# A hybrid decoder layer: a one-column GpSimd copy behind a mask product, half a low part moved from an adding transfer to VectorE, and five smaller moves of order and buffers

## The chip, the cores and the metric

The kernel runs on one core of a Trainium2 chip. The metric is the time of one execution in microseconds on the device, as the median of the runs. Its engines are TensorE (PE, matrix products), VectorE (DVE), ScalarE (ACT), GpSimd (POOL) and SyncE (SP, which only issues transfers); each has its own queue of instructions and they wait for each other by semaphores.

## What is computed

One step of a decoder layer for a prompt of 512 tokens and eight samples of eight tokens each, which share all weights. Cut to what matters here:

```python
def hybrid_layer(x, ...):
    u = _rms(x) * g_pre_mix
    proj = u @ w_in                       # 1024 -> z, xbc, dt, q, k, v, ig, fg, og
    xbc, conv_new = causal_conv(xbc, conv_buf, conv_w, conv_b)
    xs, bm, cm = split(silu(xbc))
    y_ssd, h_new = ssd_scan(xs, dt, a, bm, cm, h_ssm)      # Mamba2
    y_ssd = _rms((y_ssd + d_skip * xs) * silu(z)) * g_ssm_out
    h_ml, c_new, n_new, m_new = mlstm_scan(q, k, v, i_pre, logf, mc, mn, mm)
    h_ml = _rms(h_ml) * g_mlstm_out * sigmoid(og)
    x = x + _rms(concat([y_ssd, h_ml]) @ w_out) * g_post_mix
    o = softmax((_rms(x) * g_pre_x @ w_xq) @ mem_k.T / 16) @ mem_v @ w_xo
    x = x + _rms(o) * g_post_x
    f = (silu(u @ w_gate) * (u @ w_up)) @ w_down           # u = _rms(x) * g_pre_ffn
    return x + _rms(f) * g_post_ffn, ...
```

In `ssd_scan` the weights of one chunk are `cb * exp(segment sums, masked) * dt`; the states `h` of the samples are scaled by their decay and get one outer product added.

## The kernel before

Tokens lie in columns: 576 of them, as halves of 256 and 320. Every float32 weight tile of 128 x 1024 is split into a high part (`whi`, a cast) and a low part (`wlo`, the weight less the high part), and every product is three: high times high, high times the low part of the input, low times high (lines 208, 209 and 211 for most). A scheduler sets the order of each engine's instructions from the order of the code; `tc.issue_after(x)` places what is inside behind `x` in that order, without adding a wait of its own. An engine waits where the data or a buffer demand it.

The places that the change touches, in order of time:

- **Start** (lines 306 to 350). `NWARM` products on zeros run on TensorE while the first loads come. SP issues `par` (a table of scales), then for each of eight steps pieces of two weight tiles (`raw`) and of the input (`xraw`). ScalarE makes `uh`, the scaled input's high part, VectorE `ul`.
- **Input tiles.** `split_w` (line 178) loads a tile to `raw`, casts it on ScalarE and makes the low part: columns up to `cut` by a subtraction on VectorE, the rest, where `acc` is set, by ScalarE writing the negated high part to `wlo` and a transfer on GpSimd's queue that adds the weight to it from memory. `in_tile` (line 393) calls it by `fetch`. `conv_tile(j)` uses `in_tile(1 + j, ev, 0)`: cut 0, all by the adding transfer. `gate_tile` (line 433) runs ahead of `conv_tile(4)`, which takes input tile 5: it copies 40 rows twice out of each PSUM buffer (`xg`, `la`) on ScalarE.
- **Rows** (lines 520 to 620). Cumulated sums of the gates as rows, `cum`, `gpr`, `sx`, which TensorE then transposes (`ps_ct`). Copies in bfloat16 pieces go to `cumst` and `sxst`; `d1t` is what is left after a piece.
- **Chunk masks** (`ssd_prompt`, line 622). For each pair of heads `j`: TensorE spreads a row over PSUM (`ps_l`), VectorE adds the column term and the mask in four instructions (line 670), ScalarE takes the exponential, VectorE multiplies by `cbs` (line 673, listed in `mults`), and TensorE uses both masks of the pair in `ps_yi`. Meanwhile, in the code that follows, GpSimd scales the samples' states (`h`, line 789, two of 128 x 1024 for each `b`), after TensorE has read them for `ps_hs`; for `b == 2` that call stands in `issue_after(mults[7])`. The masks `mults[6]` and `mults[7]` are those of `j=3` in the first group.
- **z tiles** (`z_evac`, line 1050): VectorE multiplies a z tile's PSUM by the norm's row, first half and second half.
- **Memory weights** (`wm_split`): four more tiles are loaded to the shared `raw` buffers, of which there are two, and split.
- **Output projection of the attention** (`xo`, line 1529). Eight tiles for the first half of the columns, each in a PSUM buffer of the pool `pg`, which has three in turn; weights are in three `whi`/`wlo` buffers. An evacuation is a square and a sum (`add_sq`) and a scaled copy to `f_xo`, both on ScalarE but for the sum. Tile `j` takes its buffers behind the evacuation of tile `j - 3`.

Of the kernel before, what the change touches and what calls it, by code (L numbers as in the profile page):

```python
# [11 lines left out]
F32 = mybir.dt.float32  # L12
F32R = mybir.dt.float32r
BF16 = mybir.dt.bfloat16
AF = mybir.ActivationFunctionType
ALU = mybir.AluOpType
# [3 lines left out]
P = 128  # L20
# [4 lines left out]
KT = 8  # L25
# [81 lines left out]

CUT = 512
CCUT = 128
NWARM = 21  # L110
NSS = 7
NWX = 3
TCOPT = dict(schedule_with_timeline_sim=True)
# [2 lines left out]
def build(nc, tc, ctx, I, O):  # L116
# [190 lines left out]
    psw = MP("ps_warm")  # L307
    for _ in range(NWARM):
        mm(psw[:, 0:256], wz[:, 0:128], wz, start=True, stop=True, skip_group_check=True)
    S.dma_start(par, I["par"])  # L310

    wl = [wp.tile([P, 1024], F32R, name="wlo", tag="wlo", bufs=3) for _ in range(2)]
    RT = {k: wp.tile([P, 3], F32, name=k + "_r", tag=k + "_r") for k in ("px0", "p30", "px1", "p31")}
# [2 lines left out]
    for k in range(KT):  # L316
        if k % 2 == 0:
            c = slice(128 * k, 128 * k + 256)
            S.dma_start(raws[0][:, c], I["win"][1][:, c])
        xd = (S if k else A).dma_start(xraw[:, k, :], I["xT"][:, k, :])  # L320
        if k % 2 == 0:
            xd = (S if k else A).dma_start(raws[1][:, c], I["win"][2][:, c])
        if k == 0:
            with tc.issue_after(xd.ins), tc.high_priority(offset=300):

                A.activation(sp.tile([P, 1], F32, name="one"), wz[:, 0:1], AF.Exp)

        if k == 0:
            V.tensor_copy(wi[0][0][:, c], raws[0][:, c])
        for t0, n in ([(0, T)] if k else HALVES):  # L330
            ts_ = slice(t0, t0 + n)
            uhk = A.activation(uh[:, k, ts_], xraw[:, k, ts_], AF.Copy, scale=PAR("g_pre", k))
            ulk = V.scalar_tensor_tensor(ul[:, k, ts_], xraw[:, k, ts_], PAR("g_pre", k), uh[:, k, ts_].bitcast(F32),
                                         op0=ALU.mult, op1=ALU.subtract)
        if k % 2 == 0:
            for i in range(2):
                with tc.issue_after(uhk.ins), tc.issue_after(ulk.ins):
                    split(wi[i][0][:, c], wi[i][1][:, c], raws[i][:, c], cast=None if k or i else lambda *_: None)
# [123 lines left out]
    def conv_tile(j, dst):  # L462

        cb = cv.tile([P, 604], F32, name="cb", tag="cb", bufs=2)
        sm = cb[:, CS:CB].rearrange("p (b t) -> p b t", t=11)

        def ev(t0, n, ps):
            V.tensor_tensor(cb[:, 3 + t0:259 + t0], ps[:, 0:256], rxb[:, t0:t0 + 256], op=ALU.mult)
            if t0:
                V.tensor_tensor(sm[:, :, 3:11], ps[:, 256:320].rearrange("p (b t) -> p b t", t=8),  # L470
                                rxb[:, TP:T].rearrange("p (b t) -> p b t", t=8), op=ALU.mult)

        in_tile(1 + j, ev, 0)
        with ExitStack() as after:
            if 4 <= j < 10:
                for i in range(2 + j, 4 + j):
                    if i > last_in[0]:
                        fetch(i, 0)
                        last_in[0] = i
                after.enter_context(tc.issue_after(accs[-1].ins))  # L480
            if late_rows:
                late_rows.pop()()
            G.memset(cb[:, 0:3], 0.0)
            G.tensor_copy(sm[:, :, 0:3], cst[:, j, :, :])

        def rows_out():
            G.tensor_copy(convo[:, j, 0:3], cb[:, CS - 3:CS])
            G.tensor_copy(convo[:, j, 3:27].rearrange("p (b t) -> p b t", t=3), sm[:, :, 8:11])

        late_rows.append(rows_out)  # L490
        e = V
        ac = cv.tile([P, 604], F32, name="ac", tag="ac", bufs=2)
        A.activation(ac[:, 0:600], cb[:, 0:600], AF.Identity, scale=PAR("convw", 4 * j), bias=PAR("convb", j))
        for k in range(1, 4):
            e.scalar_tensor_tensor(ac[:, 0:600], cb[:, k:600 + k], PAR("convw", 4 * j + k), ac[:, 0:600],
                                   op0=ALU.mult, op1=ALU.add)
        A.activation(dst[:, 0:TP], ac[:, 0:TP], AF.Silu)
        sa = ac[:, CS:CB].rearrange("p (b t) -> p b t", t=11)
        A.activation(dst[:, TP:T].rearrange("p (b t) -> p b t", t=8), sa[:, :, 0:8], AF.Silu)
# [58 lines left out]
    V.tensor_copy(mp[r4, 512:576].rearrange("p (c t) -> p c t", t=8), m0.unsqueeze(2).to_broadcast([4, 8, 8]))  # L558
    sx = row("sx", tag="la")
    V.tensor_tensor(sx[r4, :], cum[r4, :], mrw[r4, :], op=ALU.subtract)  # L560
    V.tensor_tensor(sx[r4, :], sx[r4, :], mp[r4, :], op=ALU.add)
    V.tensor_tensor(gpr[r4, :], ig[r4, :], cum[r4, :], op=ALU.subtract)
    V.tensor_tensor(gpr[r4, :], gpr[r4, :], mp[r4, :], op=ALU.subtract)
    r2 = row("r2", 4, tag="i2")
# [7 lines left out]
    for st_, src, n in ((cumst, cum[0:16, :], 16), (sxst, sx[r4, :], 4)):  # L572
        b0 = 32 if n == 4 else 0
        bt, d1 = btt[b0:b0 + n, :], d1t[b0:b0 + n, :]
        G.memset(st_, 0.0)
        V.tensor_copy(bt, src)
        A.copy(st_[0:n, :], bt)
        V.tensor_tensor(d1, src, bt, op=ALU.subtract)
        V.tensor_copy(bt, d1)
        A.copy(st_[32:32 + n, :], bt)  # L580
        V.tensor_tensor(d1, d1, bt, op=ALU.subtract)
        A.copy(st_[64:64 + n, :], d1)
# [41 lines left out]
    def ssd_prompt(g):  # L624
# [35 lines left out]
        for j in range(4):  # L660
# [3 lines left out]
            for k in range(2):  # L664
                h = 2 * jj + k
                psb = MP("ps_l")
                mm(psb, sel[:80, h:h + 1].to_broadcast([80, P]), cumst[:, 0:TP], start=True, stop=True)
                lm = sd.tile([P, 512], F32, name="lm", tag="tmp", bufs=2)
                for c in range(4):
                    V.scalar_tensor_tensor(lm[:, c * P:(c + 1) * P], psb[:, c * P:(c + 1) * P], ncum[:, c, h:h + 1],  # L670
                                           C16("maskp"), op0=ALU.add, op1=ALU.add)
                exps.append(A.activation(lm, lm, AF.Exp))
                mults.append(V.tensor_tensor(lm, lm, cbs, op=ALU.mult))
                lms.append(lm)

            for c in range(4):
                for k in (1, 0):
# [372 lines left out]
    def z_evac(j):  # L1050
        def ev(t0, n, ps):
            t = tmp()[:, 0:n]
            V.tensor_tensor(ps, ps, rxb[:, t0:t0 + n], op=ALU.mult)
            A.activation(t, ps, AF.Tanh, scale=0.5)
            V.scalar_tensor_tensor(t, t, 1.0, ps, op0=ALU.add, op1=ALU.mult)
            yj = y[:, j, t0:t0 + n]
# [163 lines left out]
    turns = list(range(len(PRE)))  # L1220

    memh = at.tile([P, 2, KT, 256], F32R, name="memhl")
    memraw = SL(1, "memraw", F32, (P, KT, 256))
    rmem_b = at.tile([P, 256], F32, name="rmem_b")
    ssqm, ssq = ssq_tile("ssqm"), ssq_tile("ssqo")
    for j in range(8):
# [42 lines left out]
    wm = [(wmh[:, 16 + 1024 * i:1040 + 1024 * i], wml[:, 48 + 1024 * i:1072 + 1024 * i]) for i in range(4)]  # L1269

    def wm_split(i):
        split_w(I["wmk"][6 + i] if i < 2 else I["wmv"][3][:, i - 2, :], to=wm[i])

    def chain2(i, js):

# [249 lines left out]
    evx = []  # L1525
    ssq = ssq_tile("ssqxo")

    def xo(j, i, pool=None):

        t0, n = EHALVES[i]  # L1530

        with tc.issue_after(evx[j - 3].ins if j > 2 else ovs[5].ins):
            ps, w = GP("ps_xo")[:, :n], weights(("xo", j), I["wxo"][j], pool=pool, cut=1024)

        def step(k0, k1):
            m = gemm(ps, [(*w, KT)], act(oh), act(ol), t0, n, k0, k1, [2, 3, 4, 5, 6, 7, 0, 1], 6 if j == 3 else 0)
            if k1 < KT:
                return m
            add_sq(ph, ssq, ps, j if i == 0 else XO1.index(j), n, t0=t0)
            evx.append(A.activation(f[:, j, t0:t0 + n], ps, AF.Copy, scale=PAR("g_postx", j)))  # L1540
            return m, evx[-1]
        return step

    u3_ = SL(3, "u3h", F32R, (P, 5120))
# [848 lines left out]
```

## Time and profile before

| | us |
|---|---|
| runs, median (lowest, highest) | 1080.54 (1079.46, 1083.1) |
| the profiled execution, its own time | 1079.74 |
| its span, first to last instruction | 1078.0 |
| TensorE busy | 1068.0 |
| VectorE busy | 752.0 |
| ScalarE busy | 608.1 |
| GpSimd busy | 231.0 |
| mean granted TensorE clock | 0.999 |

The profiled execution is one execution beside the three timed runs; 1.7 us of its time lie outside the span. Products are pipelined, so one's listed duration is longer than the distance to the next.

### The profile page before, as it was taken

How to read it: one execution, taken by the hardware profiler on the slowest of the kernel's cores; microseconds unless marked ns; L12 is line 12 of the kernel's file. 1: busy time of each engine (PE TensorE's matmuls, PEld its weight loads, DVE VectorE, ACT ScalarE, POOL GpSimd, SP SyncE). 2: the span in 40 equal slices, each digit the busy share in tenths (PEclk: the TensorE clock that was granted, in tenths of full speed). 3: DMA queues.
4: the chain of work that ended last, by engine and by line, in shares of the span. 5: the costliest groups of instructions: out<-in, count | busy, mean ns of one | idle time of the engine just before them, and what ended most of it. 6: DMA issues, size and time to landing. Idle time of an engine off the chain costs nothing.

```text
span 1078.0 us, 20698 instructions
## 1 busy us (share of the span) xinstructions
PE 1068.0 (99%) x8124; PEld 1014.8 (94%) x8124; DVE 752.0 (70%) x1508; ACT 608.1 (56%) x1094; POOL 231.0 (21%) x304
## 2 busy tenths in 40 slices
PE   9999999999999999999999999999999999999997
PEld 9999887778999999999999989999999999999997
DVE  6897775658877775569755546766467887787556
ACT  7867522345654555556555445645567566656653
POOL 1444643313113121000154301100011111111000
PEclk9999999999999999999999999999999999999999
DMA  6786544426654438753468775743477697578532
GB/s 208 179 168 131 157 126 175 149 71 185 190 154 144 113 113 320 233 205 105 150 202 282 277 253 179 240 131 95 135 165 155 153 203 165 118 186 186 131 132 89
DMA packets 58822, 182.02 MB, mean 169 GB/s; under 512 B 6588, under 2 KB 11836, under 8 KB 58212
## 3 DMA queue, kind: packets, MB, share of 16 engines
q1 hardware_dynamic: 42740, 138.06, 39.2%
q0 software_dynamic: 15408, 41.69, 19.9%
q8 instruction: 64, 1.05, 0.4%
q10 hardware_dynamic: 576, 0.95, 0.3%
q14 instruction: 34, 0.28, 0.1%
HBM read 160.01 MB, written 20.65 MB: 168 GB/s over the span
## 4 chain that ended last, share of the span: by engine, by line
PE 95%; DVE 2%; DMA 2%; ACT 1%; issue 0%; SPq 0%; DVEq 0%; ACTq 0%
PE ps_in L208 6%; PE ps_in L211 6%; PE ps_in L209 6%; PE ps_v L850 5%; PE ps_o L211 3%; PE ps_g L1885 3%; PE ps_u L1885 3%; PE ps_g L1884 3%; PE ps_o L209 3%; PE ps_u L1886 3%; PE ps_g L1886 3%; PE ps_o L208 3%; PE ps_u L1884 3%; PE ps_dn L1884 2%; PE ps_dn L1885 2%; PE ps_dn L208 2%
## 5 line engine op out<-in xcount | busy, mean ns | idle before, releaser
L208 PE MATMUL ps_in<-uh,whi 128*128 128x320 f32 (+1 forms) x544 | 161.6, 297 | 0.3 <-ACT la L448 0.3
L211 PE MATMUL ps_in<-uh,wlo 128*128 128x320 f32 (+1 forms) x544 | 161.6, 298 | 0.0
L209 PE MATMUL ps_in<-ul,whi 128*128 128x320 f32 (+1 forms) x544 | 161.2, 296 | 0.0
L186 ACT CAST whi<-raw 128x1024 fp32r<-128x1024 f32 (+1 forms) x104 | 105.2, 1014 | 98.8 <-PE ps_in L209 25.7
L193 DVE TENSOR_TENSOR wlo<-raw,whi 128x512 fp32r<-128x512 f32 (+1 forms) x96 | 94.1, 982 | 68.7 <-ACT whi L186 67.6
L211 PEld LDWEIGHTS ps_in<-uh,wlo 128*128 128x128 f32 x544 | 102.2, 188 | 1.7 <-issue 1.3
L208 PEld LDWEIGHTS ps_in<-uh,whi 128*128 128x128 f32 x544 | 102.3, 188 | 1.4 <-ACT la L448 0.6
L209 PEld LDWEIGHTS ps_in<-ul,whi 128*128 128x128 f32 x544 | 102.3, 188 | 1.2 <-issue 0.8
L1884 PE MATMUL ps_g<-b,whi 128*128 128x288 f32 x144 | 42.4, 295 | 0.0
L1885 PE MATMUL ps_g<-b,whi 128*128 128x288 f32 x144 | 42.4, 295 | 0.0
L1885 PE MATMUL ps_u<-b,whi 128*128 128x288 f32 x144 | 42.2, 294 | 0.0
L1884 PE MATMUL ps_u<-b,whi 128*128 128x288 f32 x144 | 42.2, 294 | 0.0
L191 POOL DMA_DIRECT2D wlo<-win x31 | 26.9, 866 | 71.1 <-ACT wlo L190 66.6
L198 DVE TENSOR_TENSOR wlo<-sw,whi 128x1024 fp32r<-128x1024 f32 (+1 forms) x26 | 29.6, 1140 | 16.7 <-ACT whi L197 16.6
L1857 ACT CAST whi<-rawx 128x1024 fp32r<-128x1024 f32 (+1 forms) x26 | 25.6, 987 | 26.5 <-PE ps_dn L1885 13.7
L208 PE MATMUL ps_xo<-qh,whi 128*128 128x288 f32 x128 | 38.3, 302 | 0.2 <-ACT whi L186 0.2
L209 PE MATMUL ps_xo<-ql,whi 128*128 128x288 f32 x128 | 37.8, 297 | 0.0
L211 PE MATMUL ps_o<-mixm_h,wlo 128*128 128x256 f32 (+1 forms) x128 | 37.7, 295 | 0.0
L209 PE MATMUL ps_o<-mixm_l,whi 128*128 128x256 f32 (+1 forms) x128 | 37.5, 293 | 0.0
L211 PE MATMUL ps_xq<-u2h,wlo 128*128 128x320 f32 (+1 forms) x128 | 37.5, 294 | 0.0
L209 PE MATMUL ps_xq<-u2l,whi 128*128 128x320 f32 (+1 forms) x128 | 37.4, 294 | 0.0
L211 PE MATMUL ps_o<-mixs_h,wlo 128*128 128x320 f32 (+1 forms) x128 | 37.4, 292 | 0.0
(769 smaller groups left out, 3841.1 us busy)
## 6 DMA issues: line engine op xcount, KB each, us to landing
raw<-win SPq DMA_DIRECT2D x35, 512.0 KB, 4.2
raw<-wout SPq DMA_DIRECT2D x17, 512.0 KB, 3.7
raw<-wxq SPq DMA_DIRECT2D x13, 512.0 KB, 4.3
raw<-wgate SPq DMA_DIRECT2D x13, 512.0 KB, 3.6
raw<-wup SPq DMA_DIRECT2D x13, 512.0 KB, 5.3
wlo<-win POOLq DMA_DIRECT2D x23, 256.0 KB, 5.3
kva<-vc SPq DMA_DIRECT2D x11, 512.0 KB, 6.1
raw<-wv SPq DMA_DIRECT2D x10, 512.0 KB, 4.0
```

What stands on the lines that cost most here:

```text
L186: casts.append(A.copy(hi[:, :n], raw[:, :n]))
L191: accs.append(G.dma_start(lo[:, a:b], src[:, a:b], accum_op=ALU.add))
L193: e.tensor_tensor(lo[:, a:b], raw[:, a:b], hi[:, a:b].bitcast(F32), op=ALU.subtract)
L198: (eng or V).tensor_tensor(lo, src, hi.bitcast(F32), op=ALU.subtract)
L208: mm(ps, wh, ah, start=i == 0, stop=False)
L209: mm(ps, wh, al, start=False, stop=False)
L211: m = mm(ps, tiles[order[c]][1], xh(order[c], t0, n), start=False, stop=c == len(tiles) - 1)
L850: mm(ps, a, b, skip_group_check=True, **kw)
L1857: A.copy(s.h3[:, s.all], s.r2[:, s.all])
L1884: mm(ps, wh, b[0][k], start=start and k == 0, stop=False, skip_group_check=True)
L1885: mm(ps, wh, b[1][k], start=False, stop=False, skip_group_check=True)
L1886: m = mm(ps, wl, b[0][k], start=False, stop=k == nk - 1, skip_group_check=True)
```

## The change

Seven edits, in the order of the program:

1. 17 warming products instead of 21.
2. The load of `par` is issued behind the first weight piece.
3. Input tile 5 (`conv_tile(4)`) is fetched with `cut=512`: half of its low part by VectorE, and ScalarE's negated copy and the adding transfer are half as wide.
4. The first subtraction for `d1t` is placed behind the last of `sx`.
5. After `mults[7]` GpSimd copies one column of that mask to a tile that nobody reads; and of the first z tile the second half's multiplication is placed behind `mults[15]`.
6. The slot of `memraw` is made wider by two slices of 1024 columns; `wm_split` loads to them instead of to the shared `raw`.
7. In `xo` the evacuations of tiles 0 to 2 in the first half are kept back until tile 3 has placed its weights.

```diff
-NWARM = 21
+NWARM = 17
...
-    S.dma_start(par, I["par"])
...
+        if k == 0:
+            S.dma_start(par, I["par"])
         xd = (S if k else A).dma_start(xraw[:, k, :], I["xT"][:, k, :])
...
-        in_tile(1 + j, ev, 0)
+        in_tile(1 + j, ev, CUT if j == 4 else 0)
...
-    V.tensor_tensor(sx[r4, :], sx[r4, :], mp[r4, :], op=ALU.add)
+    sx_done = V.tensor_tensor(sx[r4, :], sx[r4, :], mp[r4, :], op=ALU.add)
...
-        V.tensor_tensor(d1, src, bt, op=ALU.subtract)
+        with tc.issue_after(sx_done.ins):
+            V.tensor_tensor(d1, src, bt, op=ALU.subtract)
...
                 mults.append(V.tensor_tensor(lm, lm, cbs, op=ALU.mult))
                 lms.append(lm)
+                if len(mults) == 8:
+                    G.tensor_copy(sd.tile([P, 1], F32, name="lm0"), lm[:, 0:1])
...
-            V.tensor_tensor(ps, ps, rxb[:, t0:t0 + n], op=ALU.mult)
+            with tc.issue_after(mults[15].ins) if t0 and j == 0 else ExitStack():
+                V.tensor_tensor(ps, ps, rxb[:, t0:t0 + n], op=ALU.mult)
...
-    memraw = SL(1, "memraw", F32, (P, KT, 256))
+    mem1 = SL(1, "memraw", F32, (P, 4608))
+    memraw = mem1[:, 0:2048].rearrange("p (k t) -> p k t", t=256)
+    spare = [mem1[:, a:a + 1024] for a in (2048, 3072)]
...
     def wm_split(i):
-        split_w(I["wmk"][6 + i] if i < 2 else I["wmv"][3][:, i - 2, :], to=wm[i])
+        with tc.issue_after(loads[-1].ins):
+            loads.append(S.dma_start(spare[i % 2], I["wmk"][6 + i] if i < 2 else I["wmv"][3][:, i - 2, :]))
+        split(*wm[i], spare[i % 2])
...
+    kept_back = []
...
+        if (j, i) == (3, 0):
+            with tc.issue_after(ends[0].ins):
+                weights(("xo", j), I["wxo"][j], cut=1024)
+            while kept_back:
+                kept_back.pop(0)()
...
-            add_sq(ph, ssq, ps, j if i == 0 else XO1.index(j), n, t0=t0)
-            evx.append(A.activation(f[:, j, t0:t0 + n], ps, AF.Copy, scale=PAR("g_postx", j)))
-            return m, evx[-1]
+            at_e = len(evx)
+            evx.append(None)
+
+            def out():
+                add_sq(ph, ssq, ps, j if i == 0 else XO1.index(j), n, t0=t0)
+                evx[at_e] = A.activation(f[:, j, t0:t0 + n], ps, AF.Copy, scale=PAR("g_postx", j))
+
+            if j < 3 and i == 0:
+                kept_back.append(out)
+            else:
+                out()
+            return m, evx[at_e]
```

The edits also move instructions that they don't name, since the scheduler orders everything anew. VectorE around the masks of `j=3` (lm, `cbs` the other factor; h are the samples' states, wlo a weight tile's low part). Before:

```order
191 L670 SCALAR_TENSOR_TENSOR lm<-ps_l,ncum,c_84 128x128 x4
192 L193 TENSOR_TENSOR wlo<-raw,whi 128x1024
193 L670 SCALAR_TENSOR_TENSOR lm<-ps_l,ncum,c_84 128x128 x4
194 L673 TENSOR_TENSOR lm<-lm,cbs 128x512
195 L793 TENSOR_TENSOR h_1936<-h_1936,ps_hu 128x512
196 L673 TENSOR_TENSOR lm<-lm,cbs 128x512
```

With the change (lines are four to five further down there):

```order
192 L797 TENSOR_TENSOR h_1935<-h_1935,ps_hu 128x512
193 L672 SCALAR_TENSOR_TENSOR lm<-ps_l,ncum,c_84 128x128 x8
194 L193 TENSOR_TENSOR wlo<-raw,whi 128x1024
195 L675 TENSOR_TENSOR lm<-lm,cbs 128x512 x2
196 L797 TENSOR_TENSOR h_1936<-h_1936,ps_hu 128x512
```

The two mask products now follow each other, behind wlo; one addition to h went ahead of the masks.

GpSimd at the same place, with the change; before it had the same rows without the copy of lm:

```order
111 L793 TENSOR_TENSOR h_1964<-h_1964,vt_1793 128x1024
112 L793 TENSOR_TENSOR h_1963<-h_1963,vt_1793 128x1024
113 L678 COPY lm_1542<-lm 128x1
114 L697 TENSOR_TENSOR xs<-xs,ec 128x384
115 L650 TENSOR_TENSOR xe<-xdt,wend 128x512
```

The copy (113) stands behind the pair of scalings for `b == 2` (111 and 112).

ScalarE at the first tiles of the output projection. Before:

```order
538 L197 CAST qh<-ps_ov 128x512 x2
539 L270 ACTIVATE ssqxo<-ps_xo 128x288
540 L1540 ACTIVATE f_xo<-ps_xo,par 128x288
541 L186 CAST whi<-raw 128x1024
542 L274 ACTIVATE sq<-ps_xo 128x288
543 L1540 ACTIVATE f_xo<-ps_xo,par 128x288
```

With the change:

```order
537 L197 CAST qh<-ps_ov 128x512 x2
538 L186 CAST whi<-raw 128x1024
539 L270 ACTIVATE ssqxo<-ps_xo 128x288
540 L1560 ACTIVATE f_xo<-ps_xo,par 128x288
541 L274 ACTIVATE sq<-ps_xo 128x288
542 L1560 ACTIVATE f_xo<-ps_xo,par 128x288
```

The cast of tile 3's weights went ahead of tile 0's evacuation (ssqxo and f_xo).

## The prediction

> **What bounds the kernel now.** I read the page's busy line first, then the waits of TensorE alone, then the timeline around each of those waits.
>
> ```profile
> PE 1068.0 (99%) x8124; PEld 1014.8 (94%) x8124; DVE 752.0 (70%) x1508; ACT 608.1 (56%) x1094; POOL 231.0 (21%) x304
> ```
>
> TensorE is busy for 1068.0 of 1078.0 us. The change removes no product of the program and adds none: only warming products, copies and positions change. So a gain can come only out of the few microseconds in which TensorE stands or warms up. These are its waits over the whole span, in the columns engine, line, what it waited for, total us, times and longest:
>
> ```profile
> PE ps_yi L678 <- DVE lm L673: 1.1, 1, 1.1
> PE ps_warm L309 <- DVE wz L306: 1.1, 1, 1.1
> PE ps_in L208 <- ACT la L448: 0.3, 1, 0.3
> PE ps_xo L208 <- ACT whi L186: 0.2, 1, 0.2
> ```
>
> Four waits, of which the change touches three; the second is the launch. The view counts a product as busy while it drains, so I price waits by start-to-start distances, which are a little longer. Nothing else is listed for TensorE, so the edits near 240 us (half of a z tile moved behind `mults[15]`) and 400 to 480 us (memory weights into spare slices) have no wait to remove. I cost them at nothing: TensorE's queue of products hides them now. Both only loosen a buffer or move one VectorE product ahead.
>
> **The mask product (1.27 us).** The timeline, columns start, duration, engine and group:
>
> ```profile
> 167.97 0.39 PE L667 MATMUL ps_l<-cumst,c 80*128 80x512 bf16 x1
> 168.41 1.12 DVE L670 SCALAR_TENSOR_TENSOR lm<-ps_l,ncum,c 128x128 f32<-128x128 f32 x4 [2.58 <-PE ps_l L667]
> 169.45 1.21 DVE L193 TENSOR_TENSOR wlo<-raw,whi 128x1024 fp32r<-128x1024 f32 x1
> 171.32 1.07 PE L781 MATMUL ps_hs<-h,cpad 128*32 128x512 f32 x8
> 171.62 0.68 DVE L673 TENSOR_TENSOR lm<-lm,cbs 128x512 f32<-128x512 f32 x1
> 172.54 4.27 POOL L789 TENSOR_TENSOR h<-h,vt 128x1024 f32<-128x1024 f32 x2 [6.21 <-PE ps_hs L781]
> 172.81 2.21 DVE L673 TENSOR_TENSOR lm<-lm,cbs 128x512 f32<-128x512 f32 x1
> 173.35 0.39 PE L850 MATMUL ps_v<-wlo,uh 128*128 128x512 f32 x1
> 173.58 0.40 PE L792 MATMUL ps_hu<-stb,bm 96*128 96x512 f32 x1
> 175.07 0.33 PE L678 MATMUL ps_yi<-lm,xdt 128*64 128x128 f32 x2 [1.10 <-DVE lm L673]
> ```
>
> The second product of the pair lasts 2.21 us where the first lasts 0.68: it began at 172.81, while GpSimd's h scaling (172.54) held what both need. TensorE issued ps_hu at 173.58 and ps_yi at 175.07, 1.49 us apart, where the product ahead (173.35) was followed after 0.23: about 1.27 us lost.
>
> In the new order the addition of ps_hu no longer stands between the two products, and the low part (wlo) stands ahead of both. The copy of one column that is to make GpSimd wait comes behind the h pair on its queue, so it holds back only what follows: xs and then xe, which have over 1 us to spare. Whether the pair is late enough is therefore decided by who gets there first. I count from the start t of the second ps_l. VectorE's additions follow the first ps_l, 0.93 ahead of t, by 0.44 (167.97 to 168.41); four take 1.04 until the next start, so the second group starts near t+0.55 and ends at t+1.6, then wlo (1.14 until the next start, 1.21 less the overlap) at 2.75, two products of 0.60, the second with its full 0.68, at 3.35 and 4.05. TensorE's own work from t to ps_yi is 13 products of v at 0.23, ps_l and ps_hu at 0.23 each and 1.07 for ps_hs: 4.5. That leaves 0.4 us of slack, if GpSimd doesn't cut in. It asks 1.2 us after ps_hs starts (171.32 to 172.54), in the new order near t+2.4, while VectorE holds wlo. Who is next when wlo ends? These rows have the same situation:
>
> ```profile
> 120.97 1.38 POOL L753 TENSOR_TENSOR lms<-lms,c 64x512 f32<-64x512 f32 x1 [1.89 <-DVE lms L752]
> 131.57 1.27 DVE L673 TENSOR_TENSOR lm<-lm,cbs 128x512 f32<-128x512 f32 x2
> 131.80 2.08 POOL L753 TENSOR_TENSOR lms<-lms,c 64x512 f32<-64x512 f32 x1 [4.44 <-DVE lms L752]
> ```
>
> At 131.80 GpSimd asked in the middle of two mask products that follow each other without a gap. Both ran undelayed (1.27 for two) and GpSimd took 2.08 instead of 1.38: it was let in only after the second. At 172.81 the instruction ahead of the product was the ps_hu addition, which reads PSUM, and GpSimd got in. So a train of instructions that read SBUF twice, without gaps, keeps what it holds. The three of the new order form such a train, because both exponentials, one ScalarE instruction each, follow the additions directly and end before wlo does. I take the whole 1.27 as gained; the bounds are 1.27 and, if GpSimd is let in, a loss that is worked out below.
>
> [...]
>
> The j=2 step of the same loop becomes tighter. Its products start 0.145 us apart:
>
> ```profile
> 159.18 0.31 PE L211 MATMUL ps_in<-uh,wlo 128*128 128x320 f32 x1
> 159.32 0.31 PE L208 MATMUL ps_in<-uh,whi 128*128 128x320 f32 x1
> ```
>
> From its second ps_l to ps_yi TensorE now has 23 of them, ps_l and two ps_hu of 0.23: 4.0 us. VectorE has a q/k evacuation ahead, eight additions (2.08), one ps_hu addition and two products (0.60 each), with the start 0.1 to 0.3 behind t: 4.0 to 4.2.
>
> I put +0.15 there (0 to 0.4). Steps j=0 and j=1 keep about 1 us of slack by the same count, though four h scalings now overlap the second pair of products.
>
> **The start and the gate tile (0.41 us).**
>
> ```profile
> 1.06 4.66 PE L309 MATMUL ps_warm<-wz 128*128 128x256 bf16 x21 [1.06 <-DVE wz L306]
> 4.77 0.29 DVE L329 CAST whi<-raw 128x256 fp32r<-128x256 f32 x1 [0.68 <-DMA raw<-win]
> 5.38 0.56 PE L349 MATMUL ps_in<-uh,whi 128*128 128x256 f32 x1
> 6.42 0.28 PE L350 MATMUL ps_in<-ul,whi 128*128 128x256 f32 x1
> 6.54 0.31 PE L349 MATMUL ps_in<-uh,whi 128*128 128x320 f32 x1
> 30.65 0.69 DVE L193 TENSOR_TENSOR wlo<-raw,whi 128x512 fp32r<-128x512 f32 x1
> 30.65 0.63 ACT L190 ACTIVATE wlo<-whi 128x512 fp32r<-128x512 f32 x1
> 33.24 1.05 ACT L186 CAST whi<-raw 128x1024 fp32r<-128x1024 f32 x1 [1.96 <-DVE cb L470]
> 35.77 1.04 ACT L190 ACTIVATE wlo<-whi 128x1024 fp32r<-128x1024 f32 x1
> 37.04 0.31 PE L444 MATMUL ps_in<-ul,whi 128*40 128x320 f32 x1
> 37.22 0.37 ACT L448 COPY la<-ps_in 40x256 f32<-40x256 f32 x1
> 37.64 0.39 PE L208 MATMUL ps_in<-uh,whi 128*128 128x256 f32 x1 [0.29 <-ACT la L448]
> ```
>
> Four warming products of 0.21 us fewer (1.06 to 5.38 for the 21, less what the last one drains) and the first weights ahead of par on SP's queue: the warm-up ends near 4.7 instead of 5.4, and the first weights, cast at 4.77 to 5.06 now, come some 0.4 earlier. The first real product moves from 5.38 to about 4.75. ScalarE and VectorE, however, follow their loads, not TensorE, up to the gate tile. There TensorE waits for the release of a PSUM buffer: xg and la are copied out behind wlo (35.77 to 36.81), 0.37 each; la ends at 37.59 and TensorE goes on at 37.64. Whatever it gained before is given back there. What moves the release is the other edit: wlo at half width takes 0.63 (the row at 30.65) instead of 1.04, so it comes 0.41 earlier, at 37.23, while a TensorE without the saved warm-up would want the buffer at 37.19 (0.15 behind 37.04). The other half costs VectorE 0.69 in a stretch where it waits for ScalarE: the cast ends at 34.29, and then come two scalings for ac until 35.77, 0.74 each, before VectorE has work; the half fits in ahead of the first one's end (34.3 to 35.0). Without that cover it would cost its 0.69 on VectorE and nothing on TensorE, since ac is used much later. GpSimd's adding transfer halves and starts earlier. Gain 0.41; bounds 0.2 and 0.45.
>
> **The row section near 79 us.**
>
> ```profile
> 75.54 0.73 DVE L578 TENSOR_TENSOR d1t<-cum,btt 16x576 f32<-16x576 f32 x1
> 78.86 0.67 ACT L566 COPY r<-sx 4x576 f32<-4x576 f32 x1
> 79.69 0.27 PE L587 MATMUL ps_ct<-c,r 100*128 100x100 f32 x1
> ```
>
> One 0.73 us subtraction goes behind sx, and ps_ct comes three products (0.43) earlier beside the 0.41 just gained. ps_ct came 0.16 behind the end of the copy; both move by 0.7 to 0.85. I put 0 (0 to +0.2).
>
> **The output projection (nothing).**
>
> ```profile
> 635.32 0.41 ACT L270 ACTIVATE ssqxo<-ps_xo 128x288 f32<-128x288 f32 x1 [2.99 <-PE ps_xo L211]
> 635.63 0.49 ACT L1540 ACTIVATE f_xo<-ps_xo,par 128x288 f32<-128x288 f32 x1
> 636.01 1.05 ACT L186 CAST whi<-raw 128x1024 fp32r<-128x1024 f32 x1
> 636.57 0.29 PE L211 MATMUL ps_xo<-qh,wlo 128*128 128x288 f32 x1
> 637.12 0.40 PE L208 MATMUL ps_xo<-qh,whi 128*128 128x288 f32 x1 [0.25 <-ACT whi L186]
> ```
>
> TensorE loses 0.41 at 636.57 (0.55 to the next start where 0.13 is usual) to the cast of tile 3, which follows the evacuation of tile 0. The change casts first and evacuates afterwards. But tile 3 takes the PSUM buffer of tile 0 (three are in turn), so its first product now waits for f_xo instead. The cast can't start before tile 0's products end at 635.3, since it overwrites their weights. The sum of ScalarE's work is the same: 635.32 plus about 1.0, 0.3 and 0.5 until the buffer is free at 637.1. I take no gain; the bounds are 0 and 0.41.
>
> **The sum.** 1.27 + 0.41 - 0.15 = 1.5 us less than the profiled execution's 1079.74, thus 1078.2. Of the three runs shown the median is 1080.54, 0.8 above it; on that scale 1079.0. I predict the middle, 1078.6.
>
> **The rivals.** The slower one: GpSimd gets the port at the end of wlo. Its first scaling then holds it for some 1.65 us (the 2.21 of the delayed product less 0.6), the first mask product ends at t+5.0, and if it is let in again ahead of the second, that ends near t+7.3: TensorE waits 2.85 instead of 1.27. With 0.41 gained and 0.15 lost that makes +1.3, 1081.1. It decides if VectorE stands for a moment between wlo and the products, as ahead of 172.81; the row at 131.57 speaks against it. Chance 0.08. Let in once only, ps_yi waits 1.24 and the edit gives nothing, so that the change doesn't do what it says: 1079.5, chance 0.13.
>
> The clock: TensorE took 0.21 us for 256 columns in the warm-up and 0.12 from 6.42 on (to 6.54), 5.3 us after the first warming product. Two or three gaps near 5 us (the second weight tile is cast later) could start that count anew. Half speed for 5.3 us more costs 2.65, of which 0.6 was saved; the gate then goes on at 39.2, 1.6 late, and the total is +0.5: 1080.2, chance 0.07. [...]
>
> Everything gained, the 0.41 of the projection too and no loss at j=2: 1077.6, chance 0.08. A new wait of about 1 us in the shuffled order of 107 to 182 us: 1079.2, chance 0.09. My forecast has 0.55.
>
> **How the numbers follow.** A measurement of this kernel tells from no change what differs by 0.3%, 3.2 us; every case above lies inside. What is outside comes from the scatter of the runs shown (1079.46 to 1083.1): faster 0.12, within 0.80, slower 0.08. The range goes from the best case with the lowest run's 1.1 below the median (1076.4) to the slower rival on the median's scale (1081.9).
>
> **What would show it.** Among TensorE's waits ps_yi on lm should fall below 0.3, the one on la below 0.1, the one in ps_xo should stay but name f_xo. Both products of the last step should last 0.68 with h behind them. Wrong are: a product over 1 us there, full clock after 7 us, a time under 1076.4 or over 1081.9.

## The result, and the profile after

| | before | changed |
|---|---|---|
| median of 22 runs each, us | 1080.47 | 1079.09 |
| lowest to highest | 1079.26 to 1083.94 | 1077.59 to 1083.06 |
| the profiled execution, its own time | 1079.74 | 1079.13 |
| its span | 1078.0 | 1077.4 |

The ratio is 0.9985, with a 95% interval of [0.9978, 0.9992]: 1.6 us less, between 0.9 and 2.4 (the two medians lie 1.4 apart), and less than the 3.2 us that were taken for no change. The prediction said 1078.6 with a sum of 1.5 us. The two profiled executions differ by 0.6 only; the one of before lies 0.7 below its median.

The busy line of the changed kernel and TensorE's waits (engine, line, what was waited for, total us, times, longest):

```profile
PE 1067.5 (99%) x8120; PEld 1015.1 (94%) x8120; DVE 752.0 (70%) x1509; ACT 607.8 (56%) x1094; POOL 231.5 (21%) x305
PE ps_warm L309 <- DVE wz L306: 1.1, 1, 1.1
PE ps_in L350 <- ACT uh L333: 1.0, 1, 1.0
PE ps_ct L589 <- ACT r L567: 0.3, 1, 0.3
```

The waits of ps_yi, of the gate tile and of ps_xo for its weights are gone from the list, and two new ones stand there. A wait is only part of it. Beside the warming products both executions make the same 8103 recorded products in another order. I gave each kind of product its mean distance to the next one over both traces, summed these as the work done, and subtracted the two starts at equal work:

| place in the program | changed less before, us | change there | predicted |
|---|---|---|---|
| first product | +0.54 | +0.54 | 0 by the gate |
| end of the half rate, about 11 us | +2.16 | +1.62 | 0 |
| behind the gate tile, 40 us | +1.58 | -0.58 | -0.41 |
| behind ps_ct, 87 us | +2.04 | +0.46 | 0 |
| 87 to 127 us | +1.96 | -0.08 | 0 |
| 127 to 153 us (ps_hs of b=1) | +0.41 | -1.55 | not in the sum |
| j=2, to 167 us | +0.73 | +0.32 | +0.15 |
| behind the masks of j=3, 177 us | -0.45 | -1.18 | -1.27 |
| 250 us (z) | -0.60 | -0.15 | 0 |
| the end | -0.61 | -0.01 | 0 |

A positive number is a loss. The sum of the predicted column is -1.53, that of the changes -0.61, the difference of the two profiled spans. The rows at the start, at ps_ct and at ps_hs are far from what was predicted, with both signs. The last row includes the output projection. Inside a stretch whose order has changed the method is good to about 0.1.

**The masks of j=3.** The timeline of the changed kernel (start, duration, engine and group), VectorE, GpSimd and TensorE:

```profile
171.43 1.21 DVE L193 TENSOR_TENSOR wlo<-raw,whi 128x1024 fp32r<-128x1024 f32 x1
172.34 5.20 POOL L793 TENSOR_TENSOR h<-h,vt 128x1024 f32<-128x1024 f32 x2 [5.25 <-PE ps_hs L785]
172.56 1.29 DVE L675 TENSOR_TENSOR lm<-lm,cbs 128x512 f32<-128x512 f32 x2
174.31 0.40 PE L854 MATMUL ps_v<-wlo,uh 128*128 128x512 f32 x1
174.63 1.09 PE L682 MATMUL ps_yi<-lm,xdt 128*64 128x128 f32 x16
```

GpSimd asked at 172.34 (its row starts there), in the middle of wlo, and both products that follow took 1.29 together; GpSimd's pair needed 5.20 where it had needed 4.27, which I read as 0.93 for which it was kept out. ps_yi follows 0.32 behind the product ahead of it, with no wait listed for its masks.

**The start.** First ghalf and uh of before, the two that read par, then the changed kernel:

```profile
3.71 0.17 DVE L413 TENSOR_SCALAR ghalf<-par 128x8 f32<-128x8 f32 x1 [2.70 <-DMA par<-par]
4.05 0.96 ACT L332 ACTIVATE uh<-xraw,par 128x256 fp32r<-128x256 f32 x2
```

```profile
1.06 3.81 PE L309 MATMUL ps_warm<-wz 128*128 128x256 bf16 x17 [1.06 <-DVE wz L306]
4.50 0.29 DVE L330 CAST whi<-raw 128x256 fp32r<-128x256 f32 x1 [3.50 <-DMA raw<-win]
5.29 0.17 DVE L414 TENSOR_SCALAR ghalf<-par 128x8 f32<-128x8 f32 x1 [0.49 <-DMA par<-par]
5.35 0.96 ACT L333 ACTIVATE uh<-xraw,par 128x256 fp32r<-128x256 f32 x2 [2.19 <-DMA par<-par]
5.91 1.09 PE L350 MATMUL ps_in<-uh,whi 128*128 128x256 f32 x2 [1.04 <-ACT uh L333]
10.16 0.35 PE L351 MATMUL ps_in<-ul,whi 128*128 128x256 f32 x1
10.35 0.28 PE L352 MATMUL ps_in<-uh,wlo 128*128 128x256 f32 x1
```

par comes 1.6 us later, and uh, which is scaled by it, comes 1.30 later; the weights, cast 0.27 earlier than before, were not what was missing. TensorE stood for 1.04, and products ran at half rate, 256 columns every 0.21 to 0.24 us instead of 0.12, until 10.35 instead of 6.42.

**The gate tile.** ScalarE and TensorE in the changed kernel:

```profile
35.20 1.05 ACT L186 CAST whi<-raw 128x1024 fp32r<-128x1024 f32 x1 [2.97 <-PE ps_in L209]
37.73 0.61 ACT L190 ACTIVATE wlo<-whi 128x512 fp32r<-128x512 f32 x1
38.75 0.37 ACT L449 COPY la<-ps_in 40x256 f32<-40x256 f32 x1
39.20 0.31 PE L445 MATMUL ps_in<-ul,whi 128*40 128x320 f32 x1
39.35 0.28 PE L208 MATMUL ps_in<-uh,whi 128*128 128x256 f32 x1
```

wlo takes 0.61 instead of 1.04, and TensorE goes on 0.15 behind its last product: no wait. But the cast at 35.20 now waited for TensorE, and stands 1.96 later than before. What was lost at the start was thus not made up here.

**The eight ps_hs of b=1.** The groups of before, then of the changed kernel:

```profile
144.43 1.05 PE L781 MATMUL ps_hs<-h,cpad 128*32 128x512 f32 x4
145.41 0.50 PE L792 MATMUL ps_hu<-stb,bm 96*128 96x512 f32 x1
145.84 1.05 PE L781 MATMUL ps_hs<-h,cpad 128*32 128x512 f32 x4
146.82 0.39 PE L211 MATMUL ps_in<-uh,wlo 128*128 128x256 f32 x1
```

```profile
145.60 1.06 PE L785 MATMUL ps_hs<-h,cpad 128*32 128x512 f32 x8
146.60 0.39 PE L208 MATMUL ps_in<-uh,whi 128*128 128x256 f32 x1
```

Four take 0.98 until the next product, and eight take 1.00. In the trace's single starts, the eight of the kernel before at 142.02 begin as four within 0.02 us and four more 0.45 later; of the four at 144.43 two begin together and two 0.45 later. So the next round came after the same 0.45, with two products as with four. The two halves with ps_hu between them cost 2.39 (144.43 to 146.82); together they cost 1.00, and ps_hu elsewhere 0.23: 1.16 less. The other 0.4 of the table's row belongs to the changed order ahead of it and wasn't traced to one place. No view of waits shows any of it, since TensorE is busy throughout.

**ps_ct and the output projection** in the changed kernel:

```profile
80.52 0.67 ACT L567 COPY r<-sx 4x576 f32<-4x576 f32 x1
80.69 0.31 PE L208 MATMUL ps_in<-uh,whi 128*128 128x320 f32 x1
81.33 0.28 PE L589 MATMUL ps_ct<-c,r 100*128 100x100 f32 x1 [0.34 <-ACT r L567]
```

```profile
634.73 1.05 ACT L186 CAST whi<-raw 128x1024 fp32r<-128x1024 f32 x1 [2.86 <-PE ps_xo L209]
635.99 0.49 ACT L1560 ACTIVATE f_xo<-ps_xo,par 128x288 f32<-128x288 f32 x1
636.11 0.29 PE L211 MATMUL ps_xo<-qh,wlo 128*128 128x288 f32 x1
636.53 0.40 PE L208 MATMUL ps_xo<-qh,whi 128*128 128x288 f32 x1
```

ps_ct stands three products earlier and the copy of sx came as late as ever beside TensorE, so 0.64 lie ahead of it where 0.15 would do. In the projection 0.42 lie where 0.13 would do, and the end of f_xo (636.48) now sets it.

### The profile page after: what moved, and what is told of

Same layout as the page of the kernel before. It is cut to its first block, busy times and chain, and to the rows that moved or that the text cites. A ratio compares the mean times of both kernels' runs of the same rounds, so it can differ in the third digit from the quotient of the medians.

```text
span 1077.4 us, 20699 instructions
## 1 busy us (share of the span) xinstructions
PE 1067.5 (99%) x8120; PEld 1015.1 (94%) x8120; DVE 752.0 (70%) x1509; ACT 607.8 (56%) x1094; POOL 231.5 (21%) x305
## 3 DMA queue, kind: packets, MB, share of 16 engines
q8 instruction: 64, 1.05, 0.4%
## 4 chain that ended last, share of the span: by engine, by line
PE 93%; DVE 3%; ACT 1%; DMA 1%; issue 1%; POOL 0%; DVEq 0%; SPq 0%; ACTq 0%
PE ps_in L208 6%; PE ps_in L211 6%; PE ps_in L209 6%; PE ps_v L854 5%; PE ps_o L211 3%; PE ps_g L1910 3%; PE ps_g L1909 3%; PE ps_o L209 3%; PE ps_g L1911 3%; PE ps_o L208 3%; PE ps_u L1910 3%; PE ps_u L1911 3%; PE ps_u L1909 3%; PE ps_dn L1909 2%; PE ps_dn L1910 2%; PE ps_dn L1911 2%
## 5 line engine op out<-in xcount | busy, mean ns | idle before, releaser
L193 DVE TENSOR_TENSOR wlo<-raw,whi 128x1024 fp32r<-128x1024 f32 (+2 forms) x97 | 94.8, 979 | 61.8 <-ACT whi L186 57.3
```

The source lines that it names most:

```text
L193: e.tensor_tensor(lo[:, a:b], raw[:, a:b], hi[:, a:b].bitcast(F32), op=ALU.subtract)
```

## The experiments

No kernel leaves out any work of the layer. Ratios are to the kernel before on the same chip; the runs stand on three chips, so a profile is compared with the profile of before only place by place.

**1. The old start** (edits 1 and 2 undone).

```diff
-NWARM = 17
+NWARM = 21
+    S.dma_start(par, I["par"])
...
-        if k == 0:
-            S.dma_start(par, I["par"])
```

> The changed kernel with the start undone: 21 warming products, par loaded first. Theory A (the start cost about 2.1 us, and nothing behind it gives that back): first product near 5.4, 256 columns in 0.12 us from about 6.5 on, the time 2.0 to 2.4 us under the changed kernel, so near 0.997 of before (-3.0 us or so). Theory B (as predicted, whatever happens at the start is swallowed at the gate tile): the same time as the changed kernel, 0.9985 of before, and a wait of 0.4 or more at the gate tile.

Measured: 1077.57, ratio 0.9967 [0.9954, 0.9979]; half rate until 5.87, TensorE 0.2 behind the kernel before at 40 us and 2.07 ahead of it at the end. Theory A in the main: nothing is swallowed at the gate, where no wait is left. At 20 us the profiles lie 2.0 apart. From 40 us on only 1.4 to 1.5 of that is left, since TensorE in this execution lost 0.6 between 24 and 27 us, where its weight loads waited for ssqx and for wlo (0.29 each). The kernel before, as early there, lost nothing, so this differs from execution to execution.

**2. 17 warming products, par first** (edit 2 undone).

> The changed kernel with par loaded first again, but 17 warming products. uh is written from about 4.05 on as before, the first product is at 5.1 and the warm-up ends at 4.5 to 4.7, a gap near 0.5. Theory A1 (a gap of half a microsecond doesn't start the clock's count anew): full rate from about 6.4 on, the time as with 21 products or 0.3 less. Theory A2 (it does): half rate until 9 or 10, 1.5 to 2 us more than with 21 products.

Measured: 1078.2, ratio 0.9971 [0.9961, 0.9981]. TensorE waited 0.39 for uh and had full rate from between 6.30 and 6.50 on: A1. This profile brought something that no theory had, TensorE behind the transposes of ps_ct and then a window of it (us, busy time and instructions of PE, PEld, DVE, ACT, POOL, then granted clock, DMA share, GB/s):

```profile
81.26 0.19 PE L593 MATMUL ps_ct<-c,r 4*64 4x4 f32 x1
81.38 0.49 PE L209 MATMUL ps_in<-ul,whi 128*128 128x320 f32 x1
81.67 0.47 PE L211 MATMUL ps_in<-uh,wlo 128*128 128x320 f32 x1
84.87 0.37 PE L211 MATMUL ps_in<-uh,wlo 128*128 128x320 f32 x1
85.08 0.28 PE L208 MATMUL ps_in<-uh,whi 128*128 128x256 f32 x1
82.00:86.00 4.00, 4.00 (x22) 4.00 (x22) 3.88 (x8) 3.78 (x8) 1.24 (x4) 0.63 0.68 143
```

From 81.38 to 85.0 products of 320 columns follow each other every 0.267 instead of 0.146: the clock fell to half for 3.5 us, which costs some 1.6. The products of this run stand in the same order as those of run 1, whose profile shows nothing of the kind.

**3. Half the low part alone** (before with edit 3 only).

```diff
-        in_tile(1 + j, ev, 0)
+        in_tile(1 + j, ev, CUT if j == 4 else 0)
```

> The kernel before with only the fifth input tile's low part halved. Theory A (this edit alone reorders the masks and puts the ps_hs products of one step together, so that it carries the gains at the gate, 0.4, of the eight ps_hs, 1.2, and of the mask product, 1.2): about -2.5 us, 0.9977 of before, no wait of ps_yi. Theory B (its worth is the gate tile alone): -0.4 us, and the mask's wait of 1.1 stays.

Measured: 1079.96, ratio 0.9985 [0.9976, 0.9994]. The mask's wait is gone and the eight ps_hs stand together, with none of the other six edits: A in mechanism. Compared place by place, TensorE's order differs from the changed kernel's in 26 of 8103 products, and in run 4, below, from that of before in 28. The size fell short, since this execution had the half rate behind ps_ct too (82.2 to 85.3), and at 454 to 468 us TensorE waited for wlo and ssqm; its lead of 0.85 at 400 us was a lag of 0.08 at 500. It also waited 0.4 for ps_ct, as the changed kernel does.

**4. All but half the low part** (edit 3 undone).

> The changed kernel with the fifth tile's low part as before, all else kept. Theory A: ps_yi waits about 1.1 for its mask as before, though the GpSimd copy is there, the eight ps_hs stand apart, and the start costs 2.1 less the 0.4 that the gate swallows: +1.5 to +2 us against before. Theory B (the copy brings the mask's gain): no wait of ps_yi, +0.5 us or less.

Measured: 1082.47, ratio 1.0007 [0.9998, 1.0015]. TensorE's waits:

```profile
PE ps_in L350 <- ACT uh L333: 1.2, 1, 1.2
PE ps_yi L682 <- DVE lm L675: 1.1, 1, 1.1
PE ps_in L208 <- ACT la L449: 1.0, 1, 1.0
```

The mask's wait stands as before, with GpSimd's copy in place: A. The median is 1.0 over that of before, less than the 1.5 expected, though the interval reaches 1.6. Against my expectation the gate swallowed nothing: TensorE came 1.8 late and waited there longer than before, not less. In this execution the cast of tile 5 stood behind a load that landed only at 35.77, 2.5 later than the cast of before; why the load was late is open.

**5. ps_ct six products later**, with the old start (in the code, `gm` lists the products of `gemm`, and ps_ct is placed behind the 424th).

```diff
+        lct = ExitStack()
+        lct.enter_context(tc.issue_after(gm[423].ins))
         for c in range(4):
             TE.transpose(psc[:, c * 104:c * 104 + 100], r1[:, c * P:(c + 1) * P], ident[0:100, 0:100])
...
+        lct.close()
```

> The changed kernel with the old start (21 warming products, par first), and ps_ct six products later on TensorE. Theory A (in the new order ps_ct stands three products too early and waits for the copy of sx; this wait, with the little work of the transposes behind it, sometimes lets the clock fall to half for 3.5 us): no wait of ps_ct, no half rate near 81 us, 0.5 us or more under the run with the old start alone (0.9967 of before), so 0.9960 or less. Theory B (the wait is only moved to what needs ps_ct, ps_en): the same as that run, and a wait of ps_en.

Measured: 1077.3, five runs from 1076.73 to 1078.01, ratio 0.9959 [0.9947, 0.9971]. The wait of ps_ct is gone, and what needs it now waits:

```profile
85.24 0.97 PE L602 MATMUL ps_en<-CT,c32e 128*128 128x416 f32 x2 [0.18 <-ACT CT L596]
```

Between 78 and 88 us TensorE loses 0.39 to the kernel before, and in run 1 0.44, so in this pair the wait was for the most part only moved, as theory B has it; in runs 9 and 10, which place ps_ct alike, the loss is 0.23 and 0.21. The 0.37 by which TensorE is ahead of run 1 at the end came from the start (0.48 ahead at 13 us). The half rate is absent here, but also in run 1's profile, and the intervals of the two overlap: that part of A isn't shown.

**6. The eight ps_hs together, in the kernel before.**

```diff
-                mm(psh[q:q + 32, :], cpad[:, g, 4 * hb + b, :],
+                with tc.issue_after(hus[0].ins) if b == 1 else ExitStack():
+                    mm(psh[q:q + 32, :], cpad[:, g, 4 * hb + b, :],
```

> The kernel before with one edit: the eight ps_hs products of b=1 stand together behind the first ps_hu instead of four on each side of it; the masks of j=3 keep their order. Theory A (four of these products take as long as eight, since eight are on TensorE four at a time): about 1.0 us per split, with the ps_hu between 1.2: 0.9989 of before, and the wait of ps_yi of 1.1 stays. Theory B (TensorE's time is that of its products, whatever their order, as the prediction took it): no difference at this place.

Measured: 1079.07, ratio 0.9979 [0.997, 0.9988]. TensorE there:

```profile
145.16 0.40 PE L794 MATMUL ps_hu<-stb,bm 96*128 96x512 f32 x1
145.49 1.06 PE L783 MATMUL ps_hs<-h,cpad 128*32 128x512 f32 x8
146.49 0.39 PE L209 MATMUL ps_in<-ul,whi 128*128 128x256 f32 x1
```

Eight in 1.00 again, and TensorE 1.2 earlier across this place: A. The wait of ps_yi didn't stay at 1.1, it was 0.7, and the delayed product took 1.83 instead of 2.21. GpSimd had asked at 171.55, during the first product, and so got in from the start of the addition behind it (171.69), which reads PSUM:

```profile
172.29 1.83 DVE L673 TENSOR_TENSOR lm<-lm,cbs 128x512 f32<-128x512 f32 x1
```

At 170 us TensorE was 0.5 ahead (this execution had come 0.6 late to the place) and at 177 0.9; at 454 it waited for wlo and at 468 for ssqm, as in run 3, and at 500 us was 0.1 behind. That the ratio says more than the expected 0.9989 is not explained by this profile.

**7. A small PSUM product ahead of the masks**, with the old start.

```diff
+                if len(mults) == 6:
+                    V.tensor_tensor(sd.tile([P, 64], F32, name="gap"), psb[:, 0:64], lm[:, 0:64], op=ALU.mult)
                 mults.append(V.tensor_tensor(lm, lm, cbs, op=ALU.mult))
```

> The changed kernel with the old start, and a small product that reads PSUM (128x64, to a tile that nobody reads) between wlo and the two mask products of j=3; the scheduler then puts an addition of ps_hu between the two as well. Theory A (GpSimd gets in at the first VectorE instruction that reads PSUM, and a train that reads SBUF alone keeps it out): one or both mask products take 2.2 us instead of 0.68, ps_yi waits 1 to 3 us, and the time is 1 to 3 us over the run with the old start alone. Theory B (the second product was slow in the kernel before only because GpSimd came in that moment; order has no part in it): 0.2 us more for the small product, no wait of ps_yi over 0.2.

Measured: 1080.76, ratio 0.9989 [0.998, 0.9998], against 0.9967 of run 1. VectorE and GpSimd:

```profile
171.14 1.22 DVE L193 TENSOR_TENSOR wlo<-raw,whi 128x1024 fp32r<-128x1024 f32 x1
172.02 4.48 POOL L794 TENSOR_TENSOR h<-h,vt 128x1024 f32<-128x1024 f32 x2 [5.21 <-PE ps_hs L786]
172.27 0.22 DVE L675 TENSOR_TENSOR gap<-ps_l,lm 128x64 f32<-128x64 f32 x1
172.41 2.30 DVE L676 TENSOR_TENSOR lm<-lm,cbs 128x512 f32<-128x512 f32 x1
174.63 0.68 DVE L798 TENSOR_TENSOR h<-h,ps_hu 128x512 f32<-128x512 f32 x1
175.23 1.82 DVE L676 TENSOR_TENSOR lm<-lm,cbs 128x512 f32<-128x512 f32 x1
```

GpSimd asked at the same point of the work as in the changed kernel, but got in at the instruction that reads PSUM, and after the second one (174.63) again: the products took 2.30 and 1.82. Theory A. Of the distance between this profile and run 1's, 3.1, some 1.7 came here, where ps_yi waited 0.4 and 0.7; 1.6 was the half rate behind ps_ct, which this profile had as well (82.5 to 85.8), and 0.4 less was lost ahead of it.

**8. 21 warming products, par behind** (edit 1 undone).

```diff
-NWARM = 17
+NWARM = 21
```

> The changed kernel with 21 warming products instead of 17, par still behind the first weights. The first product comes near 5.9 as in the changed kernel, since uh waits for par; the warm-up now ends at 5.5, a gap of 0.3 or 0.4 instead of 1.0. Theory A (the loss of the start is the clock's, and a gap of 1.0 makes it while one of 0.4 doesn't): full rate near 6.5, a loss at the start of 0.5 instead of 2.1, 1.5 us under the changed kernel. Theory B (it is the late par that costs, through all that follows it): the same time as the changed kernel.

Measured: 1078.48, ratio 0.9974 [0.9964, 0.9984], runs from 1077.44 to 1082.12. In the one profile (the run of 1082.12, the slowest) the gap was 0.58 and the half rate held until 10.43, as in the changed kernel; it lost 2.9 more at 448 and 585 us, at waits that are not the start's. The ratio is near A's 0.9971, and its interval ends just below B's 0.9985, so the loss is most likely not paid in every execution; how often is open. A gap's length alone doesn't decide it: the profile of run 7 stood for 0.91 at the start, behind a late weight, and kept full rate from 3.98 on.

**9. Without the spare slices**, run 5 with edit 6 undone.

```diff
-        with tc.issue_after(loads[-1].ins):
-            loads.append(S.dma_start(spare[i % 2], I["wmk"][6 + i] if i < 2 else I["wmv"][3][:, i - 2, :]))
-        split(*wm[i], spare[i % 2])
+        split_w(I["wmk"][6 + i] if i < 2 else I["wmv"][3][:, i - 2, :], to=wm[i])
```

> The run with the old start and the late ps_ct, with the memory weights loaded to the shared raw buffers again. Theory A (without the spare slices a chain of loads near 450 us keeps its own time, and TensorE, 2.4 us earlier there, runs into it, as it did in the two runs without the slices): TensorE waits for wlo or ssqm between 440 and 470 us, 1 to 2.4 us are given back, 0.997 to 0.998 of before. Theory B (the slices are worth nothing, as predicted): 0.9959 as with them, and no wait there.

Measured: 1079.08, ratio 0.9978 [0.9968, 0.9987]; eleven runs from 1076.66 to 1080.29. Its waits:

```profile
PE ps_o L213 <- DVE wlo L193: 0.7, 1, 0.7
PE ps_ss L237 <- DVE ssqm L278: 0.2, 1, 0.2
```

TensorE was 1.82 ahead of before at 400 us and 0.30 at 500; run 5 kept its 2.4. Theory A: 1.5 were given back.

**10. Tile 0's copy on VectorE**, run 5 with it.

```diff
-                evx[at_e] = A.activation(f[:, j, t0:t0 + n], ps, AF.Copy, scale=PAR("g_postx", j))
+                if j or i:
+                    evx[at_e] = A.activation(f[:, j, t0:t0 + n], ps, AF.Copy, scale=PAR("g_postx", j))
+
+            if j == 0 and i == 0:
+                evx[at_e] = V.tensor_scalar(f[:, j, t0:t0 + n], ps, PAR("g_postx", j), None, op0=ALU.mult)
```

> The run with the old start and the late ps_ct, and in the output projection the scaled copy of tile 0 on VectorE instead of ScalarE. Theory A (tile 3's first product waits for both readers of tile 0's PSUM buffer, which follow the cast on ScalarE one after the other; with the copy elsewhere only the square stands behind the cast): the wait of ps_xo of 0.3 goes, 0.3 us less, 0.9957 of before. Theory B (the cast of tile 3's weights holds it): the wait stays and the time is the same.

Measured: 1077.32, ratio 0.9969 [0.9958, 0.998]. No wait of ps_xo is left, and TensorE gains 0.41 there over the kernel before: A for the place. On another chip than run 5's the ratio can't tell the two apart.

**11. Without GpSimd's copy**, the changed kernel else.

```diff
-                if len(mults) == 8:
-                    G.tensor_copy(sd.tile([P, 1], F32, name="lm0"), lm[:, 0:1])
```

> The changed kernel without GpSimd's copy of one column of the mask. Theory A (the copy stands behind the pair of scalings and holds nothing back that matters; the order of VectorE alone keeps GpSimd out): mask products of 0.68, no wait of ps_yi, the changed kernel's time, 0.9985 of before. Theory B (the copy brings the gain): a product of 2.2 and a wait of ps_yi of 1.1, 1.2 us over the changed kernel.

Measured: 1079.14, ratio 0.9984 [0.9976, 0.9993]; both products 1.29 together, no wait of ps_yi. Theory A: the copy does nothing for the masks.

This profile shows the clock differently from the changed kernel's, though the products stand in the same order. Its last warming products came every 0.11 from 4.00 on, which is full rate, then TensorE stood for 1.31. The first real products of 320 columns still came every 0.15, but from between 7.28 and 7.43 on those of 256 columns came every 0.21, half rate, until between 10.73 and 10.92. It also waited 0.83 for f_mix at 424 us.

## Why the prediction was right, and where it was not

**The mask product.** Right, in mechanism and size: 1.18 of 1.27. The train of VectorE instructions that read SBUF alone kept GpSimd out (1.29 for both products, 5.20 instead of 4.27 for GpSimd's pair), and run 7 shows the slower rival's mechanism where the train is broken by an instruction that reads PSUM: products of 2.30 and 1.82, and 1.7 lost. In the changed kernel the one that asked ahead of the products, GpSimd, came behind them (asked at 172.34, products until 173.85). What the prediction calls the port is shown by no run as such; the runs show who waited, and how long. The copy behind `mults[7]` has no part in it (run 11), and edit 3 alone gives the new order (runs 3 and 4). That it does so by changing the scheduler's times at 36 us is an argument, not shown.

**The gate tile.** Right: 0.45 of the wait went, with 0.13 around it. The statement beside it fell. "ScalarE and VectorE, however, follow their loads, not TensorE, up to the gate tile" holds at most as long as TensorE is ahead; when it was 2 us late, the cast at 35.20 waited for TensorE, and run 4 shows no absorption (there the cast followed a late load). The prediction's own row had a hint: the cast at 33.24 waited for cb, which VectorE makes out of TensorE's ps_in.

**The start.** This is the step that failed: "The first real product moves from 5.38 to about 4.75"; it moved to 5.91. The step counted the weights that came earlier and not uh, which needs the load that was moved behind them. With that the clock rival came about, which had 0.07, and one of the prediction's signs of being wrong, full clock after 7 us. The rival named gaps of the weights, not uh, as the cause, but its price was right: 1.6 late at the gate, going on at 39.2, where 1.58 and 39.35 were measured. Its total of +0.5 did not come, above all because of the gain at ps_hs, which no case had. What such a gap costs isn't set by its length alone (1.04 and 0.58 were paid for, 0.91 was not, in the changed kernel and runs 8 and 7), and that a gap starts a count anew, as the prediction supposed, is not shown. The half rate behind ps_ct began, in run 2, 74.9 to 75.1 us after the first full rate (6.30 to 6.50, and 81.38), and in run 7 78.3 to 78.7 us after it; the half rate of run 11 came 3.3 to 3.6 us after the full rate and lasted 3.3 to 3.6. What sets these times no run shows: executions of one order of products differ in them, as the profiles of the changed kernel and of run 11 do.

**TensorE's order.** "So a gain can come only out of the few microseconds in which TensorE stands or warms up" was false. It carried no number of its own, and left 1.16 of gain out of the sum (run 6): what eight products cost depends on what stands between them (2.39 with ps_hu in the middle, 1.00 together and 0.23 for ps_hu elsewhere). The rows that I quoted had half of it, ps_hs x8 in 1.07; those at 144 and 146 us, x4 in 1.05, weren't used.

**ps_ct.** Mis-sized: 0 (0 to 0.2) predicted, 0.46 measured. The step that was wrong is "both move by 0.7 to 0.85": TensorE's order moved ps_ct three products ahead as expected, but the copy of sx moved by nothing beside TensorE, since it stands behind a cast on ScalarE (79.44 to 80.49; the copy starts at 80.52). The loss belongs to the order that edit 3 gives: run 3 has it without edit 4, and run 4, with edit 4, has no wait of ps_ct.

**j=2** +0.15 predicted; ps_yi stands about 0.1 late there, and the remaining 0.2 of the row in the table are spread over changes of order. **Output projection**: as predicted, the wait changed its cause to f_xo and little came of it (0.42 between the two starts instead of 0.55, and no wait listed); run 10 confirms the cause. **Edits 6 and 5's z tile at nothing**: the second gave 0.15; runs 3 and 6, without it, gain nothing there. The first removes no wait of the kernel before, and yet without it 0.9 to 1.5 us of the earlier gain are given back at 454 to 468 us (runs 3, 6 and 9), and no profile with it loses anything there: the cover of the next limit was that TensorE came late enough.

**The total.** Against the predicted column the start was 2.16 worse, ps_ct 0.46 and j=2 0.17, and the stretch of ps_hs 1.55 better, the gate 0.17 and z 0.15. That the medians differ by as much as the sum said owes to this cancelling: in the profiled pair the gain was 0.9 short of it, and the profiled execution of before was 0.7 faster than its median. So the total came out by luck, as far as the start and ps_hs go; the mask product and the gate tile came out by their mechanism. The prediction's rivals stand on the scale of the profile and the forecast 0.4 above it, and the range's lower end, 1077.6 less 1.1, is 1076.5 and not 1076.4; neither changes any of this. A version without the start's loss and with the later ps_ct (run 5) is the best measured: 0.9959 of before, clear of the changed kernel's 0.9985, though not of run 1's 0.9967.

## What to carry to other kernels

Where a transfer is moved behind another, ask for each reader of it, not only for those of the one that goes first; and where TensorE is busy all the time, price groups of products by the distance to the next one, in the order in which they stand, since a split group can cost as much as two (here 0.98 for four ps_hs and 1.00 for eight). A wait that is absent from the profile can still be the next limit: take out half a microsecond ahead of it and look who comes late. An edit whose named part does nothing may still move a whole schedule, so undo its parts one at a time before crediting any.

## What the hardware showed beyond that

The clock fell to half in the midst of the program, with TensorE standing for no more than some 0.4 us: behind transposes with few columns and a wait ahead of them it stayed at half rate for 3.1 to 3.6 us (81.38 to 85.0 in run 2, 82.2 to 85.3 in run 3, 82.5 to 85.8 in run 7). Eight profiles have that wait listed, and three of them the half rate; of the five without it (the kernel before, runs 4, 5, 9 and 10) none has it. Run 1, with the order of run 2, doesn't show it either, so the order alone doesn't decide. That the wait is a cause is likely from these counts and not shown by one pair. Four products ps_hs on 32 columns each take as long as eight, 0.98 against 1.00, where the four start in rounds of two and the eight in rounds of four.
